# When a head's transposes are given out, and where the modulation columns are computed, in a two-layer decoder trunk

## The chip, the cores and the metric

The kernel runs on one core of one Trainium2 chip. The metric is the device time in microseconds (us) of one execution; a kernel's time is the median of its runs. The engines are named as the profile names them: PE is TensorE's matmul, PEld its weight load, DVE is VectorE, ACT is ScalarE, POOL is GpSimd, SP is SyncE, whose queue issues the loads here.

## The reference

Two decoder layers on 256 tokens of width 2048, in f32. Layer 0 mixes tokens by multi-scale retention with 8 heads, layer 1 by a short gated convolution; each is followed by a SwiGLU feed-forward network (FFN) with an inner width of 5632. Shift, scale and gate of each of the four sub-layers come from a conditioning vector `c`:

```python
c_act = jax.nn.silu(c)
for i in range(DEPTH):                       # DEPTH = 2
    mod = (c_act @ w_mod[i] + b_mod[i])[:, None, :]
    sh1, sc1, g1, sh2, sc2, g2 = jnp.split(mod, 6, axis=-1)
    h = rms_norm(x, norm1_g[i]) * (1.0 + sc1) + sh1
    y = retention_mixer(h, ...) if i == 0 else short_conv_mixer(h, ...)
    x = x + g1 * y
    h = rms_norm(x, norm2_g[i]) * (1.0 + sc2) + sh2
    x = x + g2 * ((jax.nn.silu(a) * b) @ ffn_w_out[i])   # a, b = halves of h @ ffn_w_in[i]
return rms_norm(x, final_g)
```

In the retention each head's output `o` is normalised over its 512 columns, multiplied by `silu(g)`, and the 8 heads together go through the matrix `ret_w_out`.

## The kernel before

**Weights and their order.** All large weights lie in one array `w_all`, in the order of their use, as tiles of 128 x 2048 (1 MB). A *unit* of work is one block of 128 x 128 weights. Each f32 weight tile is split into a high and a low part: `prepare` lets ACT cast 1024 columns to `hi` (L416) and DVE subtract, `lo = raw - hi` (L419), into one of five places (`PLACES`). TensorE multiplies with both: `product` (L469, L472) for output columns by 256 tokens, `thrice` (L482 to L484) for 512-wide columns by 128 tokens. `take` hands the next block to TensorE and calls `prepare` as long as a place is free.

**Order on the engines.** TensorE's order is the order in which the program gives its instructions out, and so it is written out by hand. DVE, ACT and POOL are ordered by the framework's scheduler, from the order of the program and its priorities. All loads go through the SP queue in order.

**The retention.** For each head, in the order of `HEAD_ORDER` (4, 0, 2, 1, 5, 3, 6, 7), `projections` multiplies q and k (two columns of 128, so two units a step), v (512 columns, four units a step) and the gate. What remains of the head (`mixed`) is put into the list `asides` and given out within the *next* head's products: `outputs(0)`, then `last_outputs`, which ends with `normed_outputs` (a root of sums on DVE and the power on POOL, L581 and L583, then `o` for two halves of the tokens on DVE, L1073), then `ends`: eight 128 x 128 transposes of `o` on TensorE (L1084) into two banks, and four casts (L548) and four subtractions (L549) that split the result into `mid`. `ticked` counts the units given out, and an aside leaves when its number in `STEPS` is reached; the count then starts again. After every fourth head `ret_out` multiplies `mid` by half of `ret_w_out`; its first product has six columns, six units a step, and it is there that the fourth and the eighth head's asides are given out.

**The modulations.** The `modulation` of one block of 128 columns loads 1 MB of `w_mod` through SP into one of the four `raw` buffers, which it shares with `w_all` (`RAW_BUFS`), multiplies it by `cb` (the conditioning vector on all partitions) and sums, on DVE (L323), at a low priority (`MOD_PRIO`), and adds bias and gain on POOL. 192 are computed: 32 at the very start and 160 (`n_mod`) along the way. For the latter `plan_mod` lists pairs of units given out and modulations due by then, and between two pairs `paced` interpolates; no more than 0.08 are given out per unit (`MOST`). `needed` gives out at once what is still missing where a column is used.

**Units.** Retention and its output matrix take units 0 to 2048. The first FFN is done in two parts: its input matrix for 20 of 44 tiles (2048 to 2688), the output matrix for these (2688 to 3008), the input for the other 24 (3008 to 3776) and their output (3776 to 4160). The convolution's input follows (to 4928), its output (to 5184), and then the second FFN.

**The FFN's input matrix.** It is taken in groups of four tiles, 128 units each, in eight pairs of rows of 16 units (`gathered`). In three pairs of each group (`FFN_SEVEN`) seven products stand in for eight (`sevens`), for which DVE makes differences of weight blocks ahead of the split (L403, L407, L409); `mixed_sums` (L1208 to L1212) gathers the four banks of these after the last of them, and TensorE's first product of the next group needs a bank that L1212 reads.

The two places that the change touches:

```python
STEPS = (8, 8, 20)
...
            return list(zip(STEPS, [lambda: outputs(0), last_outputs, ends]))
...
    plan_mod = [(early, 0), (1024, 28), (1984, 72), (2688, 84), (3008, 96), (3776, 106), (5184, n_mod)]
```

Of the kernel before, what the change touches and what calls it, by code (L numbers as in the profile page):

```python
# [47 lines left out]
MOD_LEAD = 64  # L48
MOST = 0.08
MOD_PRIO = -300  # L50
STEPS = (8, 8, 20)
RAW_BUFS = 4
PLACES = 5
FETCHED, PLAIN, WARM, ADDED = 2, 3, (5, 0, 0, 0, 0, 0, 0, 8), ()
# [207 lines left out]
def trunk(ctx: ExitStack, tc: tile.TileContext, x_in, c_in, pos_in, w_mod, cols_in, gain_in, tab_in, w_all, out):  # L262
# [76 lines left out]
    n_mod = len(todo)  # L339
    todo.reverse()  # L340
    first = RET_SPANS[0].n * FIRST_KS
    early = sum(g.n * len(g.ks) for g in RET_SPANS)
    plan_mod = [(early, 0), (1024, 28), (1984, 72), (2688, 84), (3008, 96), (3776, 106), (5184, n_mod)]
    units, allowed = [0], [0.0]

    def paced(n):
# [372 lines left out]
    with ExitStack() as inner:  # L719
# [331 lines left out]
        def mixed(head, both, v, sg):  # L1051
# [4 lines left out]
            def outputs(t):  # L1056

                pt = bank().rearrange("p a b -> p (a b)")
                pts.append(pt)
                n = 0  # L1060
                for jt in range(t + 1):
                    sp = both[jt][:, :, (t - jt) * P : (t - jt + 1) * P]
                    for i, j in ((0, 0), (0, 1), (1, 0)):
                        nc.tensor.matmul(pt, sp[:, i, :], v[:, jt, j, :], start=n == 0, stop=n == 3 * t + 2)
                        n += 1
                sq = rp.tile([P, DV], F32, tag="o", name=name("sq"), bufs=2)
                nc.scalar.activation(sq, pt, AF.Square, accum_out=total[:, t : t + 1])
# [23 lines left out]

            return list(zip(STEPS, [lambda: outputs(0), last_outputs, ends]))

# [453 lines left out]
```

## Time and profile before

| | |
|---|---|
| median of 3 runs | 2567.32 us (2565.79 to 2568.79) |
| the profiled execution's own time | 2568.4 us |
| its span, from the first to the last instruction | 2566.6 us |
| mean granted TensorE clock | 0.998 |
| HBM read | 685.11 MB, 268 GB/s over the span |

The profile's page gives busy time by engine; a table of waits gives, for each waiting instruction, the one that ended its wait, the total, how often, and the longest; the view by stretches cuts the span at given times; the timeline lists single instructions with their start, their length, and in brackets how long the engine had stood idle before and who ended it. Matmuls are pipelined, so each one's length in the timeline (0.39 us for 512 columns) is longer than the distance between two starts.

### The profile page before, as it was taken

To read this page: it belongs to the slowest core of one execution; us is meant where nothing else is said; L and a number is where in the kernel's file an instruction comes from. 1 tells how busy PE (TensorE), PEld (TensorE's weight loads), DVE (VectorE), ACT (ScalarE), POOL (GpSimd) and SP (SyncE) were. 2 spreads that over 40 slices of the span, in tenths; PEclk is the share of its full clock that TensorE was granted. 3 is DMA by queue.
4 is the path that set the end of the run, shared out by engine and by line. 5 is a ranking of instruction groups with operands and counts; after the bars stand their busy time and mean duration, and the time that the engine had idled before them with its cause. 6 is when DMAs were issued, how large, how long until landed. Compare 5 with 4: busy or idle time off the path is not lost.

```text
span 2566.6 us, 34867 instructions
## 1 busy us (share of the span) xinstructions
PE 2543.9 (99%) x13330; PEld 2186.1 (85%) x13330; DVE 2334.6 (91%) x2925; ACT 1346.1 (52%) x1789; POOL 178.4 (7%) x232
## 2 busy tenths in 40 slices
PE   8999999999999999999999999999999999999998
PEld 6898888888889888888888898888998888888887
DVE  7989999898899999889999888888989999999988
ACT  5544443454456555345555454444565555555554
POOL 0000111011111010000000111000000000000001
PEclk9999999999999999999999999999999999999999
DMA  9987889888876667866668878878846465555653
GB/s 398 390 331 263 309 321 340 334 300 308 329 278 234 231 261 285 322 245 227 248 230 301 302 282 309 330 292 299 317 159 214 180 229 212 181 214 182 228 197 131
DMA packets 96696, 689.48 MB, mean 269 GB/s; under 512 B 10744, under 2 KB 12168, under 8 KB 13456
## 3 DMA queue, kind: packets, MB, share of 16 engines
q1 hardware_dynamic: 96528, 687.25, 72.1%
q8 instruction: 104, 1.70, 0.3%
q14 instruction: 64, 0.52, 0.1%
HBM read 685.11 MB, written 2.11 MB: 268 GB/s over the span
## 4 chain that ended last, share of the span: by engine, by line
PE 90%; DVE 6%; DMA 2%; issue 1%; ACT 1%; ACTq 0%; SPq 0%; POOLq 0%; POOL 0%; DVEq 0%
PE bank L469 20%; PE bank L482 17%; PE bank L484 17%; PE bank L483 17%; PE bank L472 11%; DVE lo L419 2%; DMA raw<-w_all 1%; PE bank L533 1%; PE bank L664 1%; PE bank L532 1%; PE bank L666 1%; PE bank L665 1%; PE bank L531 1%; DVE raw L795 1%; DVE raw L323 1%
## 5 line engine op out<-in xcount | busy, mean ns | idle before, releaser
L416 ACT CAST hi<-raw 128x1024 fp32r<-128x1024 f32 (+1 forms) x981 | 990.5, 1020 | 932.8 <-PE bank L484 361.8
L419 DVE TENSOR_TENSOR lo<-raw,hi 128x1024 fp32r<-128x1024 f32 (+1 forms) x981 | 1143.9, 1181 | 148.3 <-ACT hi L416 143.3
L482 PE MATMUL bank<-hi,h 128*128 128x512 f32 x1540 | 602.7, 391 | 1.1 <-DVE u L1212 1.0
L483 PE MATMUL bank<-lo,h 128*128 128x512 f32 x1540 | 600.9, 390 | 0.1
L484 PE MATMUL bank<-hi,h 128*128 128x512 f32 x1540 | 600.8, 390 | 0.0
L323 DVE SCALAR_TENSOR_TENSOR raw<-raw,cb 128x2048 f32<-128x2048 f32 x160 | 365.9, 2287 | 28.9 <-DMA raw<-w_mod 28.6
L484 PEld LDWEIGHTS bank<-hi,h 128*128 128x128 f32 x1540 | 289.3, 188 | 61.2
L482 PEld LDWEIGHTS bank<-hi,h 128*128 128x128 f32 x1540 | 289.5, 188 | 59.6 <-DVE u L1212 1.9
L483 PEld LDWEIGHTS bank<-lo,h 128*128 128x128 f32 x1540 | 289.6, 188 | 58.4 <-DVE lo L419 0.8
L469 PE MATMUL bank<-h,hi 128*128 128x512 f32 x928 | 323.0, 391 | 0.0
L469 PE MATMUL bank<-mid,hi 128*128 128x512 f32 x920 | 319.4, 390 | 0.0
L472 PE MATMUL bank<-h,lo 128*128 128x256 f32 x928 | 261.3, 282 | 0.0
L472 PE MATMUL bank<-mid,lo 128*128 128x256 f32 x920 | 259.6, 282 | 0.0
L469 PEld LDWEIGHTS bank<-h,hi 128*128 128x128 f32 x928 | 174.1, 188 | 36.9
L469 PEld LDWEIGHTS bank<-mid,hi 128*128 128x128 f32 x920 | 172.7, 188 | 35.8
L472 PEld LDWEIGHTS bank<-h,lo 128*128 128x128 f32 x928 | 175.7, 189 | 0.3
L472 PEld LDWEIGHTS bank<-mid,lo 128*128 128x128 f32 x920 | 174.2, 189 | 0.1
L469 PE MATMUL bank<-rm,hi 128*128 128x512 f32 x496 | 172.5, 391 | 0.0
L472 PE MATMUL bank<-rm,lo 128*128 128x256 f32 x496 | 140.0, 282 | 0.0
L482 PE MATMUL bank<-hi,mid 128*128 128x512 f32 x297 | 116.0, 391 | 0.0
L484 PE MATMUL bank<-hi,mid 128*128 128x512 f32 x297 | 115.9, 390 | 0.0
L483 PE MATMUL bank<-lo,mid 128*128 128x512 f32 x297 | 115.7, 390 | 0.0
(281 smaller groups left out, 3430.4 us busy)
## 6 DMA issues: line engine op xcount, KB each, us to landing
raw<-w_all SPq DMA_DIRECT2D x456, 1024.0 KB, 5.0
raw<-w_mod SPq DMA_DIRECT2D x192, 1024.0 KB, 6.3
x<-x_in SPq DMA_DIRECT2D x4, 512.0 KB, 5.4
out<-xt SPq DMA_DIRECT2D x4, 512.0 KB, 3.0
decay<-tab_in SPq DMA_DIRECT2D x8, 128.0 KB, 5.3
x<-gate_row SPq DMA_DIRECT2D x2, 512.0 KB, 4.8
last_gain<-gain_in SPq DMA_DIRECT2D x1, 1024.0 KB
cols<-cols_in SPq DMA_DIRECT2D x1, 152.0 KB, 8.2
```

What stands on the lines that cost most here:

```text
L323: nc.vector.scalar_tensor_tensor(raw, raw, 1.0, cb, op0=ALU.mult, op1=ALU.mult, accum_out=total)
L416: nc.scalar.copy(hi[:, o], raw[:, o])
L419: nc.vector.tensor_tensor(lo, raw, hi.bitcast(F32), op=ALU.subtract)
L469: nc.tensor.matmul(pt, hi, h, start=fresh and k == g.ks[0], stop=False, skip_group_check=True)
L472: nc.tensor.matmul(pt[:, 1, :], lo, h[:, 0, :], start=False, stop=last and k == g.ks[-1], skip_group_check=True)
L482: nc.tensor.matmul(o, hi, w_hi, start=first, stop=False)
L483: nc.tensor.matmul(o, hi, w_lo, start=False, stop=False)
L484: nc.tensor.matmul(o, lo, w_hi, start=False, stop=last)
L531: nc.tensor.matmul(pt, hi, h[:, 0, :], start=first, stop=False, skip_group_check=True)
L532: nc.tensor.matmul(pt, hi, h[:, 1, :], start=False, stop=False, skip_group_check=True)
L533: nc.tensor.matmul(pt, lo, h[:, 0, :], start=False, stop=last, skip_group_check=True)
L664: nc.tensor.matmul(pt, hi, high, start=k == 0, stop=False, skip_group_check=True)
```

## The change

The third number of `STEPS` goes from 20 to 24, so that `ends` is given out four units later. Two numbers of `plan_mod` go down by four: 80 modulations are due at unit 2688 in place of 84, and 102 at unit 3776 in place of 106. The other pairs stay as they were, and so does the number of modulations.

```diff
-STEPS = (8, 8, 20)
+STEPS = (8, 8, 24)
...
-    plan_mod = [(early, 0), (1024, 28), (1984, 72), (2688, 84), (3008, 96), (3776, 106), (5184, n_mod)]
+    plan_mod = [(early, 0), (1024, 28), (1984, 72), (2688, 80), (3008, 96), (3776, 102), (5184, n_mod)]
```

## The prediction

> **What bounds the kernel now.** I read the page first, then the table of who waited for whom on TensorE, then busy time by stretch, then the timeline at the two places where TensorE stood still in the middle.
>
> ```profile
> span 2566.6 us, 34867 instructions
> PE 2543.9 (99%) x13330; PEld 2186.1 (85%) x13330; DVE 2334.6 (91%) x2925; ACT 1346.1 (52%) x1789; POOL 178.4 (7%) x232
> ```
>
> TensorE (PE) is the bound: 22.7 us of the span are left in which it is not busy. The table of waits (total, times, longest, in us) says where some of them lie:
>
> ```profile
> PE bank L590 <- POOL rs L922: 3.5, 1, 3.5
> PE bank L1084 <- DVE o L1073: 2.3, 2, 1.2
> PE bank L533 <- DVE lo L419: 2.0, 3, 0.9
> ...
> PE bank L482 <- DVE u L1212: 1.0, 1, 1.0
> ```
>
> L590 and L533 belong to the opening stage, which the change does not reach. L1084 are the transposes that the first edit moves; L482 after `u` of L1212 lies in the first FFN's first matrix, which the second edit relieves. The stretches (start:end, length, then busy us and count of PE, PEld, DVE, ACT, POOL, then PE clock, DMA share, GB/s) confirm that there is little else:
>
> ```profile
> 0.00:66.00 66.00, 58.38 (x268) 45.68 (x268) 47.44 (x60) 34.35 (x60) 2.87 (x5) 0.97 0.98 399
> ...
> 2500.00:2566.00 66.00, 57.71 (x254) 47.29 (x252) 56.03 (x73) 31.57 (x45) 8.18 (x8) 0.96 0.34 128
> ```
> ```profile
> 240.00:300.00 60.00, 57.67 (x281) 48.24 (x280) 57.09 (x76) 28.80 (x43) 6.45 (x7) 1.00 0.77 279
> 360.00:450.00 90.00, 90.00 (x522) 79.89 (x521) 81.68 (x97) 35.27 (x38) 13.02 (x26) 1.00 0.90 333
> 780.00:995.00 215.00, 213.84 (x1087) 181.35 (x1088) 209.58 (x278) 126.78 (x176) 20.49 (x20) 1.00 0.65 242
> 995.00:1106.00 111.00, 111.00 (x644) 98.40 (x643) 95.20 (x107) 43.61 (x44) 9.81 (x13) 1.00 0.84 312
> 1106.00:1361.00 255.00, 255.00 (x1142) 210.53 (x1141) 243.11 (x270) 142.89 (x159) 9.96 (x9) 1.00 0.65 235
> 1361.00:1497.00 136.00, 136.00 (x817) 121.89 (x816) 120.81 (x147) 65.42 (x83) 20.43 (x23) 1.00 0.82 305
> 1497.00:1765.00 268.00, 268.00 (x1638) 241.70 (x1637) 235.99 (x330) 134.60 (x204) 27.56 (x39) 1.00 0.83 304
> ```
>
> The opening 66 us lack 7.6 us of PE and the last 66 us lack 8.3; neither is touched. 780:995 is the first part of the first FFN's input matrix (with its opening columns), 995:1106 that part's output matrix, 1106:1361 the second part's input, 1361:1497 its output, 1497:1765 the convolution's input. VectorE (DVE) is busy for 97% and 95% of the two input stretches and for 86%, 89% and 88% of the other three; yet only 780:995 shows any PE idle time, 1.2 us. So in the middle of the kernel about 3.5 us can be won at most: 2.3 in 240:300 and 1.2 in 780:995.
>
> **First edit: transposes four units later.** A head's eight transposes, four ACT casts and four DVE subtractions (L548, L549) are given out after 24 units instead of 20. Nothing is added, no DMA moves, and no bank is taken in another order, since the four units never cross the end of a product. Six heads change; in the other two the next work is `ret_out` with six units a step, and both 20 and 24 are passed at its fourth step. Only one head waits now:
>
> ```profile
> 282.81 2.29 DVE L323 SCALAR_TENSOR_TENSOR raw<-raw,cb 128x2048 f32<-128x2048 f32 x1
> 283.07 2.57 POOL L583 TENSOR_TENSOR rs<-rs,half 128x2 f32<-128x2 f32 x1 [6.13 <-DVE rs L581]
> ...
> 285.01 0.39 PE L484 MATMUL bank<-hi,h 128*128 128x512 f32 x1
> ...
> 285.69 0.75 DVE L1073 SCALAR_TENSOR_TENSOR o<-bank,rs,sg 128x512 f32<-128x512 f32 x1
> ...
> 286.59 0.63 PE L1084 MATMUL bank<-tab,o 128*128 128x128 f32 x4 [1.19 <-DVE o L1073]
> 286.95 0.69 DVE L1009 TENSOR_TENSOR q<-qa,q 128x512 fp32r<-128x512 f32 x1
> 287.55 0.75 DVE L1073 SCALAR_TENSOR_TENSOR o<-bank,rs,sg 128x512 f32<-128x512 f32 x1
> ...
> 288.35 0.66 PE L1084 MATMUL bank<-tab,o 128*128 128x128 f32 x4 [1.14 <-DVE o L1073]
> ...
> 288.76 0.48 PE L482 MATMUL bank<-hi,h 128*128 128x512 f32 x1
> ```
>
> The two normalised outputs `o` come late because the small POOL power behind them runs 2.57 us beside a modulation. PE starts a 512-wide matmul every 0.23 us here (909.33 to 909.56 below), so the work after 285.01 could have begun at 285.24. The first four transposes start at 286.59, 1.35 us late. They take 0.12 us each in step, (0.63 - 0.27)/3, about 0.45 together, so the second four could go at 287.04 and go at 288.35, 1.31 late. Four units of this place are one row of the value matrix: 2 token halves x 3 matmuls x 0.23 = 1.4 us of PE work that now comes ahead of them. So the first four would start at 286.6, when the first `o` (ended 286.44) is there; the second four still wait for 288.30, since `o` does not move. Gain: 1.35 us; what is late next is the second `o`, 1.3 us. Bounds: 2.7 if both waits go, 0 if `o` slides along.
>
> The price is on ACT and DVE, whose queues hold the L548 and L549 in order:
>
> ```profile
> L549 DVE TENSOR_TENSOR rm<-bank,rm 128x256 fp32r<-128x256 f32 x32 | 12.8, 421 | 0.0
> L548 ACT CAST rm<-bank 128x256 fp32r<-128x256 f32 x32 | 11.0, 373 | 8.8 <-PE bank L1084 5.0 <-DVE rm L549 3.7
> ```
>
> Behind them stand the casts and subtractions of the next weights. At worst each of six heads holds those up for 1.4 us more, 8 us in all, if no prepared weights lay ahead; at best 0. I take 0: of the nine rows of PE's waits only that of L533 names `lo`, although ACT stands before L548 for 5.0 us already. The transposed outputs themselves are read only in `ret_out`, heads later.
>
> **Second edit: modulations.** One modulation is one DVE instruction over 2048 elements plus the read of its accumulator, one load of 1 MB (128 x 2048 of 4 bytes), and one or two tiny POOL operations:
>
> ```profile
> L323 DVE SCALAR_TENSOR_TENSOR raw<-raw,cb 128x2048 f32<-128x2048 f32 x160 | 365.9, 2287 | 28.9 <-DMA raw<-w_mod 28.6
> ...
> L323 DVE DVE_READ_ACCUMULATOR raw<-raw,cb 128x1 f32 x160 | 13.5, 84 | 0.0
> ```
>
> 2.37 us of DVE each. Their number stays 160. From unit 1984 to 2688 eight are due in place of twelve, from 2688 to 3008 sixteen in place of twelve, from 3008 to 3776 six in place of ten, and from there to 5184 fifty-eight in place of fifty-four. So about 4 x 2.37 = 9.5 us of DVE leave each input matrix; the first four go to the output matrix right behind it, the other four to the second output matrix and the convolution. The one wait they can lift:
>
> ```profile
> 901.67 2.28 DVE L323 SCALAR_TENSOR_TENSOR raw<-raw,cb 128x2048 f32<-128x2048 f32 x1
> ...
> 909.33 0.39 PE L483 MATMUL bank<-lo,h 128*128 128x512 f32 x1
> 909.56 0.39 PE L484 MATMUL bank<-hi,h 128*128 128x512 f32 x1
> 909.61 0.68 DVE L1211 TENSOR_TENSOR u<-bank,extra 128x512 f32<-128x512 f32 x1
> 910.21 0.68 DVE L1212 TENSOR_TENSOR u<-bank,u 128x512 f32<-128x512 f32 x1
> ...
> 910.95 0.50 PE L482 MATMUL bank<-hi,h 128*128 128x512 f32 x1 [1.00 <-DVE u L1212]
> ```
>
> The next group of tiles needs the bank that L1212 reads. PE starts at 910.95 instead of 909.79: 1.16 us. This group spans units 2304 to 2432; two modulations are due in it now (2336 and 2395), and with a step of 88 units instead of some 59 also two, but at 2336 and 2424, the second at the group's very end. The one at 901.67, 6 us ahead of the wait, is then gone. I take the whole 1.16 as won; ends 0 and 1.16.
>
> What hides the added ones? In 995:1106 the cast runs ahead until TensorE frees a place:
>
> ```profile
> L416 ACT CAST hi<-raw 128x1024 fp32r<-128x1024 f32 x40 | 42.1, 1053 | 67.8 <-PE bank L469 61.7 <-PE bank L472 3.7 <-PE bank L484 1.7
> ```
> ```profile
> L416 ACT CAST hi<-raw 128x1024 fp32r<-128x1024 f32 x96 | 100.8, 1051 | 97.2 <-PE bank L469 69.3 <-DMA raw<-w_all 13.8 <-issue 10.0
> ```
>
> (The second row is 1497:1765.) 62 of 68 idle us of the cast are waits for a place to come free, so prepared weights lie ahead, and DVE goes from 95.2 to about 104.7 of 111 us. Cost 0; without that cover each added modulation would cost its 2.37, 9.5 us per stretch. In the convolution the cast waits 13.8 us for its weights' load already, but the load rises by only 2 modulations in 30. Cost 0.
>
> The loads share one SP queue and four buffers with the weights. In 995:1106 the change adds 4 x 1.05 MB in 111 us, 38 GB/s: 312 becomes 350. The opening stretch moved 399, and 360:450 moved 333 with PE busy for all of its 90 us; between 0 and the price of a ceiling at 333 (below, among the rivals) I take 0, since 350 is below what the same queue has moved.
>
> The Trainium skill speaks against this: DMA: Bandwidth & Descriptors, section Bandwidth, measured 341 GB/s for a transfer of 1 MB, issued from GpSimd. By that the stretch would last 350/341 x 111 = 113.9 us, an estimate, 2.9 more than now, and the sum would be 2567.7. The 399 GB/s of the opening, moved by loads issued from SP that overlap, does not agree with 341 as a ceiling here.
>
> **Sum.** The profiled execution took 2568.4 us (span 2566.6 and 1.8 around it), 1.1 above the median of the runs, 2567.3. 2568.4 - 1.35 - 1.16 = 2565.9, which against the median is 2564.8, 0.1% less.
>
> **The rivals.**
>
> Nearly all waits go: between the two `o` DVE does other work from 286.44 to 287.55; put behind the second `o`, that saves 1.1 more. 1.35 + 1.1 + 1.16 = 3.6 less, 2563.7. For it: the order on DVE is made by a scheduler, which sees a new order on TensorE. Against: neither `o` is given out at another time, so nothing asks for it.
>
> The change does not do what it says: the scheduler lets `o` slide, or the bank's reader is late again because ACT waits for a weight load there. 0 to 1.2 less, 2566.7. For it: `o` is late because one modulation happened to run beside one POOL operation, and another order moves that elsewhere. Against: no modulation is due at another time before unit 1984.
>
> Slower, at the group ends of the second input matrix: 6 modulations in 768 units are due every 128 units, which is exactly one group of four tiles, so all six come at the borders where L1212 frees the bank for the next group. One border today:
>
> ```profile
> 1232.34 0.68 DVE L1212 TENSOR_TENSOR u<-bank,u 128x512 f32<-128x512 f32 x1
> ...
> 1255.52 2.29 DVE L323 SCALAR_TENSOR_TENSOR raw<-raw,cb 128x2048 f32<-128x2048 f32 x1
> ```
> ```profile
> 1233.33 0.39 PE L482 MATMUL bank<-hi,h 128*128 128x512 f32 x1
> ```
>
> L1212 ends 0.3 us before PE needs the bank. A modulation put ahead of it costs 2.37 - 0.3 = 2.07; six cost 12.4, less 2.5 won: 2577; with the 1.16 of the border at 909.56 each, 7.0 less 2.5: 2571.8. I take 2573. Against: unit 3392 is such a border and has a modulation due today, and it ran at 1255.52, 22 us after. It decides from four borders on.
>
> Loads: if the 333 GB/s of 360:450 were the ceiling, 995:1106 would last 350/333 x 111 = 116.7, 5.7 more: 2570.5, a loss of 0.12%. Against: the DMA share at 333 was 0.90, not 1. (The rule of the Trainium skill named above is the same mechanism with a milder ceiling.)
>
> **How the numbers follow.** Forecast 0.45; nearly all waits go 0.08; does not do it 0.19; group ends 0.22; loads 0.06. The likeliest is 2564.8, alone 2563.3 to 2566.3 by the spread of the runs (1.5 each way). The range, 2562.3 to 2572.5, holds all but the tails of the four cases below 2571, and nearly half of the group ends. 0.2% (5.1 us) is about what a measurement of this kernel can tell from no change. No case gains that much by itself; about a tenth of the forecast and a third of the second, by the spread, give 0.07 for faster. Slower takes most of the group ends and a little of the loads, 0.22. The rest, 0.71, is within.
>
> **What would show it.** L1084 should wait for `o` once, about 1.3 us, near 287 us; the wait of L482 for L1212 should be gone; PE's total idle time about 20 us. Modulations (L323) should number about 17 in 995:1106 and 5 to 7 in 1106:1361, and each of the latter should lie 5 to 25 us behind a group's end. Wrong would be: L482 waiting for `u` at several borders, `lo` appearing in TensorE's waits after 800 us, or a DMA share of 1.0 in 995:1106.

## The result, and the profile after

The changed kernel takes 2563.20 us (median of 22 runs, 2562.37 to 2565.69) against 2566.64 (22 runs, 2565.35 to 2568.79): 3.4 us less, ratio 0.9988, 95% interval 0.9982 to 0.9993. That is faster, by less than 0.2%. The forecast was 2.5 us less. The profiled execution took 2562.85 us.

The page of the changed kernel, its head:

```profile
span 2561.0 us, 34886 instructions
## 1 busy us (share of the span) xinstructions
PE 2541.6 (99%) x13330; PEld 2184.1 (85%) x13330; DVE 2334.5 (91%) x2925; ACT 1347.0 (53%) x1789; POOL 169.5 (7%) x232
```

Its table of waits on TensorE, whole (total, times, longest):

```profile
PE bank L590 <- POOL rs L922: 3.5, 1, 3.5
PE bank L533 <- DVE lo L419: 2.2, 4, 0.9
PE bank L531 <- ACT h L823: 1.3, 1, 1.3
PE bank L863 <- DVE half L303: 1.0, 1, 1.0
PE bank L892 <- DVE sq L905: 0.9, 1, 0.9
PE bank L877 <- DVE c_parts L872: 0.6, 1, 0.6
PE bank L1064 <- DVE sp L549: 0.5, 1, 0.5
PE bank L518 <- ACT u L822: 0.3, 1, 0.3
```

L1084 and L482 have both left the table; all but L1064 belong to the opening. The stretches of the changed kernel, at the same times as before (start:end, length, busy us and count of PE, PEld, DVE, ACT, POOL, then clock, DMA share, GB/s):

```profile
240.00:300.00 60.00, 60.00 (x295) 50.61 (x294) 59.39 (x79) 30.75 (x46) 7.57 (x8) 1.00 0.81 300
...
780.00:995.00 215.00, 215.00 (x1093) 183.02 (x1093) 207.34 (x276) 128.87 (x180) 16.72 (x12) 1.00 0.62 228
995.00:1106.00 111.00, 111.00 (x636) 98.13 (x635) 96.81 (x106) 41.41 (x41) 10.04 (x17) 1.00 0.89 333
1106.00:1361.00 255.00, 255.00 (x1147) 210.59 (x1146) 240.20 (x269) 145.68 (x162) 6.64 (x6) 1.00 0.62 226
```

PE is now busy in every microsecond of these. VectorE lost little in the first input stretch (209.6 to 207.3) and gained as little in 995:1106, because a stretch cut by time holds later work of a kernel that is 5 us ahead. So I cut by units instead: the time from TensorE's first multiplication by `lo` of one unit to that of another, from the records of the trace counted against the order of the weights. The first row runs from the start of the span. Stages whose time never moved by 0.2 us in these profiles are left out.

| units | before | changed | e1: 24 alone | e2b: plan alone | e4: second move alone | e5: 16 | e7: moved twice as far | e8: due at borders |
|---|---|---|---|---|---|---|---|---|
| 0 to 496, opening | 204.13 | 203.61 | 203.63 | 203.55 | 203.35 | 203.83 | 203.59 | 203.45 |
| 496 to 1024, retention | 202.25 | 199.49 | 199.49 | 199.93 | 199.95 | 201.83 | 199.55 | 199.48 |
| 2176 to 2304, a group | 42.34 | 41.89 | 42.35 | 41.87 | 42.35 | 42.33 | 41.84 | 41.85 |
| 2304 to 2432, a group | 43.01 | 42.65 | 43.04 | 42.63 | 43.01 | 43.05 | 42.65 | 42.65 |
| 2432 to 2560, a group | 43.92 | 42.63 | 43.90 | 42.63 | 43.93 | 44.35 | 42.63 | 42.63 |
| 2688 to 3008, first output | 112.05 | 111.83 | 112.05 | 111.83 | 112.05 | 112.05 | 114.42 | 111.83 |
| 3136 to 3264, a group | 42.63 | 42.67 | 42.63 | 42.64 | 43.60 | 42.63 | 42.65 | 42.65 |
| 3392 to 3520, a group | 42.63 | 42.63 | 42.63 | 42.63 | 42.63 | 42.63 | 43.56 | 42.63 |
| 3776 to 4160, second output | 134.10 | 134.10 | 134.10 | 134.10 | 134.10 | 134.10 | 134.92 | 134.10 |
| 4160 to 4928, convolution in | 268.71 | 268.71 | 268.71 | 268.71 | 268.71 | 269.13 | 268.71 | 270.37 |

The two spans differ by 5.6 us: 2.76 in the retention, 2.32 in the first part of the first FFN, and 0.52 in the opening up to unit 496, which the change does not reach. That the medians differ by 3.4 only suggests that some of this is peculiar to the executions that were profiled.

### The profile page after: what moved, and what is told of

Read it like the earlier page. It is cut to its first block, busy times and chain, and to the rows that moved or that the text cites. A ratio compares the mean times of both kernels' runs of the same rounds, so it can differ in the third digit from the quotient of the medians.

```text
span 2561.0 us, 34886 instructions
## 1 busy us (share of the span) xinstructions
PE 2541.6 (99%) x13330; PEld 2184.1 (85%) x13330; DVE 2334.5 (91%) x2925; ACT 1347.0 (53%) x1789; POOL 169.5 (7%) x232
## 4 chain that ended last, share of the span: by engine, by line
PE 96%; DVE 2%; DMA 1%; ACT 1%; issue 0%; SPq 0%; ACTq 0%; POOLq 0%; POOL 0%; DVEq 0%
PE bank L469 21%; PE bank L482 18%; PE bank L484 18%; PE bank L483 18%; PE bank L472 11%; PE bank L664 1%; PE bank L666 1%; PE bank L665 1%; PE bank L533 1%; PE bank L532 1%; PE bank L531 1%; DVE raw L795 1%; PE bank L1278 1%; DMA raw<-w_all 1%; PE bank L1064 1%; DMA raw<-w_mod 1%
## 5 line engine op out<-in xcount | busy, mean ns | idle before, releaser
L416 ACT CAST hi<-raw 128x1024 fp32r<-128x1024 f32 (+1 forms) x981 | 991.1, 1020 | 952.6 <-PE bank L484 357.4
L482 PE MATMUL bank<-hi,h 128*128 128x512 f32 x1540 | 602.0, 391 | 0.0
L482 PEld LDWEIGHTS bank<-hi,h 128*128 128x128 f32 x1540 | 289.3, 188 | 58.2
L482 PE MATMUL bank<-hi,mid 128*128 128x512 f32 x297 | 115.8, 390 | 0.0
```

The lines of the kernel that those rows point to most:

```text
L416: nc.scalar.copy(hi[:, o], raw[:, o])
L482: nc.tensor.matmul(o, hi, w_hi, start=first, stop=False)
```

## The experiments

Each edit below is against the kernel before, except where it says otherwise.

**e1_steps: the transposes alone.**

```diff
-STEPS = (8, 8, 20)
+STEPS = (8, 8, 24)
```

> Only the transposes are given out four units later (24); the modulations stay as in the kernel before. Theory: the two edits act at two places and add up, so this one takes away the waits of L1084 for o, 1.35 to 2.7 us of TensorE time, and leaves the wait of L482 for u of L1212 near 910 us (about 1.1 us). Time about 2564.5, ratio 0.9990 to 0.9995. Rival: the gain comes from the modulations alone, and the time is within 0.5 us of the kernel before.

2565.53 us against 2567.24, ratio 0.9994 (0.9986 to 1.0003): the size expected, not settled by the runs. By units the edit acts in 496 to 1024 alone, and the wait for L1212 stays, as the theory had it. The 2.76 us of that stage are measured against the one profile of the kernel before; e2b_plan below shows how much of them is the edit's.

**e2_plan, e3_first: the modulations alone, and their first move alone.** By a slip both also had two further pairs four units early:

```diff
-    ... (1984, 72), (2688, 84), (3008, 96), (3776, 106), (5184, n_mod)]
+    ... (1980, 72), (2688, 80), (3008, 96), (3776, 102), (5180, n_mod)]    # e2_plan
+    ... (1980, 72), (2688, 80), (3008, 96), (3776, 106), (5180, n_mod)]    # e3_first
```

> Only the modulations are moved (80 and 102); the transposes stay at 20 units. Theory: the wait of L482 for L1212 goes (1.16 us), the waits of L1084 stay. Time 0.8 to 1.5 us under the kernel before. Up to unit 1984 this program is the same as the kernel before, so its profile is also a second sample of the two waits of L1084: if the load that the cast waited 4.1 us for was slow by chance, the second of them is shorter here. Rival: all of the gain of 3.4 us is here, by relief of VectorE over both input matrices.

> Of the modulations only the first four are moved (80 due at unit 2688, 106 at 3776 as before), transposes at 20. Theory: this holds all that the plan gains, 0.8 to 1.5 us, as the only wait of TensorE that modulations cause lies in the first input matrix. Rival: half of the gain of the plan, the other half lying in the second input matrix.

2564.84 (0.9994, 0.9985 to 1.0003) and 2563.52 us (0.9986, 0.9977 to 0.9995), against 2567.24: 2.4 and 3.7 us less by the medians, both more than the 0.8 to 1.5 expected. Up to unit 1024, where the first pair begins to count, they are the kernel before, and in both profiles L1084 waits 0.2 us in place of 2.3.

**e4_second: the second move alone.**

```diff
-    ... (3776, 106), (5184, n_mod)]
+    ... (3776, 102), (5184, n_mod)]
```

> Of the modulations only the second four are moved (84 due at unit 2688, 102 at 3776), transposes at 20. Theory: no change, within 0.3 us of the kernel before, since TensorE has no idle time in the second input matrix to win; the wait near 910 us stays. Rival: it costs or gains over 0.5 us, through modulations at the ends of the groups of tiles or a lighter VectorE.

2567.69 us, ratio 1.0005 (0.9996 to 1.0013): no gain. By the runs the theory holds, by the stages the rival's cost is there. The profile has the old wait and a new one behind it, at the first border of the second input matrix. Its row in the table of waits, and the two DVE instructions ahead of the new one:

```profile
PE bank L482 <- DVE u L1212: 1.6, 2, 1.0
```
```profile
1138.57 2.29 DVE L323 SCALAR_TENSOR_TENSOR raw<-raw,cb 128x2048 f32<-128x2048 f32 x1
...
1147.12 0.68 DVE L1212 TENSOR_TENSOR u<-bank,u 128x512 f32<-128x512 f32 x1
```

The modulation ends 6 us ahead of L1212, as the one at 901.67 did in the kernel before, and two subtractions for weights queue up behind it. By units the group behind this border takes 0.97 us more.

**e2b_plan, e3b_first, e9_two: the same without the slip.** e2b_plan has the change's whole plan with `STEPS` at 20; e3b_first has only (2688, 80); e9_two is the changed kernel with (3776, 106) put back.

> The modulations alone, transposes at 20 units, now with nothing else changed (in e2_plan and e3_first two further pairs of the plan were four units early, 1980 and 5180). Theory after the first four runs: the plan wins its time in the first FFN part alone, 2.0 to 2.4 us between units 2176 and 3008, and the retention from unit 496 to 1024 takes 200.0 us (202.3 in the profile of the kernel before, where one load of weights took 9.0 us in place of 6.6). Rival: the 202.3 us are the rule for 20 units, and show again here.

> Only 80 due at unit 2688, transposes at 20, 106 due at 3776. Theory: the same stage times as with both moves, 41.9, 42.6 and 42.6 us for the groups that took 42.3, 43.0 and 43.9, so within 0.5 us of e2b_plan. Rival: the second move is worth over 0.7 us, and this run is slower than e2b_plan by that.

> The changed kernel without its second move: transposes at 24, 80 due at unit 2688, 106 at 3776. Theory: as fast as the changed kernel, 2563.2, ratio 0.998 to 0.9993, as the second input matrix has nothing to win. Rival: 1 us slower than the changed kernel, by a wait of L482 for L1212 at a border of the second input matrix.

2564.07 (0.9992, 0.9983 to 1.0001), 2563.99 (0.9991, 0.9982 to 1.0) and 2563.08 us (0.9988, 0.9978 to 0.9997), against 2566.59. The plan alone wins 0.47 + 0.38 + 1.29 + 0.22 = 2.36 us by units, all in the first part of the first FFN; e3b_first and e9_two have the same stage times there. So the second move is worth nothing, beside the first one, and costs nothing. And 202.25 us is not the rule for 20 units: without it stand 199.93 here and 199.95 in e4_second.

What was peculiar: in the kernel before, the cast at L416 stood 4.10 us for a load of weights. The row on ACT, and the load in the chain of waits of that stretch (start, length):

```profile
279.92 1.05 ACT L416 CAST hi<-raw 128x1024 fp32r<-128x1024 f32 x1 [4.10 <-DMA raw<-w_all]
280.87 0.59 ACT L1067 ACTIVATE sq<-bank 128x512 f32<-128x512 f32 x1
```
```profile
270.81 9.01 DMA raw<-w_all
```

Behind that cast waits L1067, the sum of squares from which `o` is normalised. In e2b_plan the same cast waits for no load, and the second four transposes wait 0.22 us:

```profile
276.67 1.05 ACT L416 CAST hi<-raw 128x1024 fp32r<-128x1024 f32 x1 [1.47 <-PE bank L484]
...
278.00 0.60 ACT L1067 ACTIVATE sq<-bank 128x512 f32<-128x512 f32 x1 [0.28 <-PE bank L1064]
```
```profile
285.44 0.66 PE L1084 MATMUL bank<-tab,o 128*128 128x128 f32 x4 [0.22 <-DVE o L1073]
```

**e5_steps16: the transposes four units earlier.**

```diff
-STEPS = (8, 8, 20)
+STEPS = (8, 8, 16)
```

> The kernel before with the transposes four units earlier (16 in place of 20). Theory: the transposes wait only where o is not there yet, by the amount that they come early; at 20 units the profiles without a slow load show 0.2 us at one head, at 24 none. Four units are 1.4 us of TensorE work, so at that head the wait becomes about 1.4 us more for each of the two halves at most, and heads whose o ends less than 1.4 us ahead of the transposes now (four of the six) add up to 1 us each: 2 to 6 us slower than the kernel before, all of it between units 496 and 2048. Rival: the second edit is all there is and the place of the transposes does not matter, within 0.5 us.

2569.22 us against 2566.51, 2.7 more by the medians; the ratio of the runs, 1.0007 (0.9998 to 1.0016), does not settle it. The profile does say where. 496 to 1024 takes 201.83 us, 1.9 more than at 20 units without the slow load. Two smaller losses lie outside the heads, where none was expected: 0.43 in the group 2432 to 2560, where L482 waits 1.4 us for L1212 in place of 1.0, and 0.42 in the convolution's input; what leads from the edit to these stays open. In the retention the wait is back:

```profile
PE bank L1084 <- DVE o L1073: 1.6, 2, 1.1
```

It is one head, the one that waits 0.2 us at 20, and not the four that I expected to join in.

**e7_less: the changed kernel with the move doubled.**

```diff
-    ... (2688, 80), (3008, 96), (3776, 102), ...
+    ... (2688, 76), (3008, 96), (3776, 98), ...
```

> The changed kernel with twice the move: 76 due at unit 2688 and 98 at 3776. Theory: the groups of the first FFN are at their floor of 42.63 us in the changed kernel, so nothing more is won: within 0.5 us of the changed kernel (2563.2). Rival: VectorE's load in the input matrices sets the time, and four more modulations taken out of each win another 1 to 2 us.

2568.45 us, ratio 1.0006 (0.9997 to 1.0014): all of the gain is lost, and both theories are wrong. By units it is 4.5 us behind the changed kernel. The groups of the first part stay at their floor, but the first output matrix takes 114.42 us, 2.6 more. Of these, 0.8 are lost in its first 16 units, and 1.8 at two later places (0.9 each, from units 2896 and 2976), where TensorE waits for `lo`. Two more losses lie in the second part: 0.9 in the group 3392 to 3520, and 0.8 in the first 16 units of the second output matrix. For the waits for `lo`, the stretch and two of its rows, of e7_less:

```profile
995.00:1106.00 111.00, 109.49 (x628) 96.42 (x628) 100.47 (x109) 38.99 (x40) 13.21 (x22) 1.00 0.91 344
```
```profile
L472 PE MATMUL bank<-mid,lo 128*128 128x256 f32 x304 | 85.9, 283 | 1.2 <-DVE lo L419 1.2
...
L416 ACT CAST hi<-raw 128x1024 fp32r<-128x1024 f32 x38 | 38.3, 1051 | 72.0 <-DMA raw<-w_all 47.9 <-PE bank L469 17.0 <-DVE lo L419 4.0
```

And the same row of the changed kernel:

```profile
L416 ACT CAST hi<-raw 128x1024 fp32r<-128x1024 f32 x39 | 40.8, 1054 | 68.1 <-PE bank L469 38.6 <-DMA raw<-w_all 28.2 <-issue 1.2
```

In the kernel before, nearly all of the cast's idle time in that stretch was a wait for a free place, the sign that it ran ahead. With 16 modulations due in this matrix 28.2 us of it are a wait for weights, and with 20 it is 47.9 and TensorE waits for `lo`. The cover was used up within one further step, at a price of 1.8 us. The other three losses, 2.6 us together, stand right behind borders of groups (2688, 3392 and 3776), and they are not the loads': ahead of each of these borders a modulation ended 2.2 us before L1209. The next experiment takes this up.

**e8_border: an attempt to make the slower rival happen.** Against the changed kernel:

```diff
-        with tc.high_priority(offset=MOD_PRIO):
+        with tc.high_priority(offset=0 if 2992 < units[0] <= 3760 else MOD_PRIO):
...
-    ... (3008, 96), (3776, 102), ...
+    ... (2992, 96), (3760, 102), ...
```

> The changed kernel, but the six modulations of the second input matrix are due 16 units earlier and at normal priority, which puts each of them a few DVE instructions ahead of L1209 at the end of a group. It makes the slower rival of the prediction happen: that one expects 1.2 to 2.1 us at each of six borders, 7 to 12 us over the changed kernel, so 2570 to 2575. Theory: TensorE waits for L1212 at each border, 0.8 to 1.2 us (0.97 where it happened by chance in e4_second), 5 to 7 us in all. If VectorE catches up before L1212, nothing is lost, and the time is 2563.

2564.31 us, ratio to the kernel before 0.9992 (0.9983 to 1.0001). The 5 to 7 us of the theory did not come. Every group of the second input matrix still takes 42.63 to 42.65 us, with a modulation on DVE that ends 3.9 to 4.5 us ahead of L1209 at each of the six borders. The edit did not bring them as close as those that cost something. Over all profiles, by how long before L1209 the last modulation ended:

| ended ahead of L1209 | where | what it goes with |
|---|---|---|
| 4.9 us and more | every border of the second part that is not named below, in all profiles; the six of the changed kernel have 13 us and more | no loss |
| 3.9 to 4.5 us | all six borders, e8_border | no loss |
| 2.2 us | border 2432 in the kernel before, e1, e4, e5 | the group behind it takes 1.3 to 1.7 us more than its floor |
| 2.2 us | border 3136 in e4, 3392 in e7 | 0.97 and 0.93 us |
| 2.2 us | borders 2688 and 3776 in e7 | 0.8 us each, in the output matrix behind it |
| not before L1209, but between it and L1212 | border 2304 in the kernel before, e1, e4, e5 | some 0.4 us in the group behind it |

So what goes with the loss is how close ahead of L1209 the modulation stands. That 4 us are enough is seen; where between 2.2 and 3.9 us the loss begins was not tested, nor why DVE's order puts a modulation there in some of these kernels.

What e8_border does lose, 1.7 us by units, it loses at the convolution's norm, where the shift of the plan put a modulation ahead of L581 on DVE. The rows on DVE, of e8_border and then of e9_two:

```profile
1495.14 2.29 DVE L323 SCALAR_TENSOR_TENSOR raw<-raw,cb 128x2048 f32<-128x2048 f32 x1 [2.76 <-DMA raw<-w_mod]
...
1498.50 0.15 DVE L581 TENSOR_SCALAR rs<-bank 128x2 f32<-128x2 f32 x1
```
```profile
1495.16 0.16 DVE L581 TENSOR_SCALAR rs<-bank 128x2 f32<-128x2 f32 x1
...
1498.85 2.28 DVE L323 SCALAR_TENSOR_TENSOR raw<-raw,cb 128x2048 f32<-128x2048 f32 x1
```

In e8_border DVE stands 2.76 us for the modulation's load and works 2.29 on it, with the norm's small L581 behind it in the queue; TensorE then waits:

```profile
PE bank L590 <- POOL rs L583: 1.4, 1, 1.4
```

## Why the prediction was right, and where its sizes were off

**Direction and total** held: 3.4 us less where 2.5 were forecast, inside the range, and less than 0.2%. The two terms of the sum were each mis-sized, and in opposite ways.

**The transposes, 1.35 us.** The prediction took both waits of L1084 for the rule and said that the second `o` would still be late. In the changed kernel neither half waits; DVE and PE there:

```profile
282.87 0.74 DVE L1073 SCALAR_TENSOR_TENSOR o<-bank,rs,sg 128x512 f32<-128x512 f32 x1
...
284.73 0.74 DVE L1073 SCALAR_TENSOR_TENSOR o<-bank,rs,sg 128x512 f32<-128x512 f32 x1
...
286.06 1.03 PE L1084 MATMUL bank<-tab,o 128*128 128x128 f32 x8
```

The order of DVE is the same as before, so the rival in which the second `o` moves ahead did not happen. The first `o` came 2.8 us earlier, 0.5 of them because the whole stretch was ahead since the opening, the rest because no load took 9.01 us. Five other profiles with 20 units show L1084 waiting 0.2 us, and against these the edit is worth 199.95 - 199.49 = 0.46 us. The prediction put the late `o` down to the POOL power of 2.57 us beside a modulation. That does not explain the 2.3 us: in e2b_plan, at 20 units, the same power takes the same 2.57 us beside a modulation, and L1084 waits 0.2. So the term was mis-sized in one step: one wait of one execution was carried into the sum without asking whether the load behind it was slow by chance. It was, in one of six. How often it is among unprofiled runs stays open, and so does what the edit wins when the load is slow.

**The modulations, 1.16 us.** The mechanism was right, the size half of what it was. Taken alone the plan wins 2.36 us: 1.29 in the group where L482 waited, and 0.47, 0.38 and 0.22 in the groups and the output matrix beside it. Those were not in the table of waits, because each is made of pauses of some 0.1 to 0.25 us between matmuls. The profile counts PE as busy through most of them, so that its idle time of 1.2 us in 780:995 was no upper bound for the gain, though I used it as one.

**The sum.** By units the two terms are 0.46 and 2.36, 2.8 us together, where 1.35 and 1.16 were forecast. That two errors in opposite ways left the sum at 2.5 is luck. The measured 3.4 is 0.6 more than the stages account for; this lies within the interval of the ratio, which is 1.8 to 4.6 us less.

**The cover in 995:1106**, cost 0: right for the changed kernel (111.83 us, 0.22 less than before), but nearer to its end than "62 of 68 idle us" made it look. I had 350 GB/s for that stretch; it was 333, with no wait on TensorE. In e7_less the rival of the loads comes true, at 344 GB/s and a DMA share of 0.91, but for 1.8 us and not its 5.7.

**The Trainium skill's** figure of 341 GB/s for one transfer of 1 MB (DMA: Bandwidth & Descriptors, section Bandwidth) lies between the 333 that did no harm and the 344 that did. But a ceiling it is not: the changed kernel's opening moves more, by loads that overlap:

```profile
66.00:110.00 44.00, 42.36 (x267) 38.05 (x268) 40.46 (x41) 24.20 (x37) 0.00 (x0) 1.00 1.01 421
```

**The group ends**, the slower rival, did not come true in the changed kernel. The six modulations come due at the borders, as worked out, and run in the middle of the next group, as the one of unit 3392 did. Two rows of DVE in the changed kernel:

```profile
1184.19 0.68 DVE L1212 TENSOR_TENSOR u<-bank,u 128x512 f32<-128x512 f32 x1
...
1207.38 2.28 DVE L323 SCALAR_TENSOR_TENSOR raw<-raw,cb 128x2048 f32<-128x2048 f32 x1
```

23 us lie between them. Moved to some 4 us ahead of L1209 they cost nothing either (e8_border). But the mechanism exists: one that ends 2.2 us ahead of L1209 goes with 0.8 to 1.0 us at one new border in e4_second and at three in e7_less. The price of 1.16 per border was about right and that of 2.07 too high. That the changed kernel pays it nowhere hangs on DVE's order, which the prediction could only weigh.

**No gain at all** was refuted by the interval of the ratio.

## What to carry to other kernels

Before a wait in a profile goes into a sum, follow it back to its source: where that is a load, look at the same load in a second execution, for it may have been slow by chance. Where the bound engine pauses for less than a microsecond, measure it by stage, from a unit of work to a unit of work, and not by its idle time. Work moved to a stage with slack is free only while the stage's preparer still waits for free places; look at what that wait turns into after the first move, before making a second. And look at where the scheduler puts what was moved: here a modulation that ended 4 us ahead of a bank's readers cost nothing, and one that ended 2.2 us ahead went with 0.8 us or more.

## What the runs showed of the hardware

The load of 1 MB behind the cast above took from 4.9 to 9.0 us in the six profiles with 20 units, whose programs are the same up to there, and the one of 9.0 us went with a wait of 2.3 us on TensorE.

By its stages the profile of e3b_first is 3.0 us longer than that of e2b_plan, all of it in units 5184 to 5312, with the last FFN's norm: 53.35 us in place of 50.37. On DVE a modulation stood for its load shortly before (of e3b_first), and the norm's sums on TensorE came late:

```profile
1841.09 2.29 DVE L323 SCALAR_TENSOR_TENSOR raw<-raw,cb 128x2048 f32<-128x2048 f32 x1 [1.74 <-DMA raw<-w_mod]
```
```profile
PE bank L569 <- ACT acc L555: 1.3, 1, 1.3
```

This wait is 1.3 of the 3.0 us. The rest is the clock: behind the wait the granted clock was 0.5 for 3.4 us, from 1855.24 us on, and TensorE's matmuls of 256 columns start 0.21 us apart in place of 0.12. PE there, of e3b_first:

```profile
1854.96 0.28 PE L664 MATMUL bank<-h,hi 128*128 128x258 f32 x1
1855.08 0.28 PE L665 MATMUL bank<-h,hi 128*128 128x256 f32 x1
...
1855.38 0.42 PE L664 MATMUL bank<-h,hi 128*128 128x258 f32 x1
1855.59 0.42 PE L665 MATMUL bank<-h,hi 128*128 128x256 f32 x1
```

At half the clock 3.4 us hold the work of 1.7. In none of the other profiles does the clock fall between 23 us and the last 10 us, not even behind the wait of 1.4 us in e8_border, so it is not shown that a wait brings this about.

The runs of each kernel, the changed one too, scatter over some 3 us, and of this both a slow load and the clock are possible causes. Of the 33 runs of the kernel before beside e1_steps, the 18 with a mean granted clock of 0.997 took 2567.9 us on average, and the 15 with 0.998 or 0.999 took 2565.8. Which of the two comes first was not tested.
